# Splitting most FFN weight blocks by casting and accumulating transfers in a two-layer encoder trunk

## The chip, the cores and the metric

The kernel runs on one core of a Trainium2 chip. The time is device microseconds of one launch. The engines are TensorE (PE; PEld is its weight load), VectorE (DVE), ScalarE (ACT), GpSimd (POOL) and SyncE (SP). SP and POOL issue DMA transfers here: SP in both versions, POOL only in the changed one.

## The reference

Two layers of an encoder on a (512, 1024) float32 input. Each layer is a gated mixer of three attention-like branches, a layer norm, a SwiGLU FFN with 2816 hidden channels, and a second layer norm. The change touches the FFN alone:

```python
u = jnp.einsum('bsd,df->bsf', x, w_ffn_in[l])
u_gate, u_up = jnp.split(u, 2, axis=-1)
ffn = jnp.einsum('bsf,fd->bsd', jax.nn.silu(u_gate) * u_up, w_ffn_out[l])
x = _layer_norm(DEEPNORM_ALPHA * x + ffn, ln2_g[l], ln2_b[l])
```

## The kernel before

Every float32 matrix product is carried out as three products of float32r parts. A value w is split into a high part, w cast to float32r, and a low part, w minus the high part. `mm3` then multiplies high by high, high by low and low by high into one PSUM bank.

The program is a list of work items. An item has one or more weight blocks (`specs`) and a function that consumes them. A block is 1 MB of float32 weights, spread over 128 partitions with 2048 values each: for the FFN's input projection 8 row groups of 128 gate columns and 128 up columns (two pieces, in runs of 512 bytes), for its output projection 4 row groups of 512 columns (one piece, in runs of 2 KB). The sixth output block of each half has 2 row groups only.

`Wt` fetches and splits a block. SP loads it into one of two stage tiles `st`, ScalarE casts it to the high part `wh` in two halves, and VectorE subtracts `wh` from `st` to make the low part `wl`. `wh` and `wl` have four buffers each (`AHEAD`), so a block can be split as soon as TensorE has read the block four before it. `run_items` fetches ahead until four blocks are ready or in use, then runs the next item. All engines take their instructions in the order in which a scheduler has put them, and wait at the head of their queue.

In layer `l` the FFN consists of these items: `u_ffn_first(2)` with the first two input blocks, `u_ffn(2)` to `u_ffn(21)` with one input block each, `u_fout(0, 0..5)` and `u_fout(1, 0..1)` with one output block each, and `u_fout_last` with the last four. A full block is 48 matmuls of 512 columns on TensorE. After an input block, `ffn_done` forms the hidden channels: a tanh and a cast on ScalarE, three operations on VectorE. The norm ahead of the FFN (`normalise`) takes one power per 128 rows on POOL; the transposes of the normed rows (`px`) wait for it, and `u_ffn_first` needs them.

Of the kernel before, what the change touches and what calls it, by code (L numbers as in the profile page):

```python
# [12 lines left out]
F32R = mybir.dt.float32r  # L13
AF = mybir.ActivationFunctionType
ALU = mybir.AluOpType

P = 128
# [32 lines left out]
def trunk(ctx, tc, x_in, w_in, ret_norm_g, da_norm_g, lq1, lk1, lq2, lk2, w_a, w_b, w_c, b_merge, w_out,  # L50
          ln1_g, ln1_b, w_ffn_in, w_ffn_out, ln2_g, ln2_b, rel, rope_ret, rope_da, decay, out):
    nc = tc.nc
# [5 lines left out]
    wsp = ctx.enter_context(tc.tile_pool(name="wsp", bufs=AHEAD))  # L58
# [9 lines left out]
    def g(dt=F32, name="g"):  # L68
        return gp.tile([P, 512], dt, tag="g", name=name)

    def f(ap):
        return ap.bitcast(F32)

    def bank(name="ps"):
        return psp.tile([P, 512], F32, tag="ps", name=name)

    class Pair:


        def __init__(self, name="pr"):  # L80
            self.hi = g(F32R, name + "h")
            self.lo = g(F32R, name + "l")
# [23 lines left out]
    class Wt:  # L106


        def __init__(self, pieces, nk, meanwhile=None):
            ncol = sum(ap.shape[1] for ap in pieces)  # L110
            n = nk * ncol
            st = wst.tile([P, 2048], F32, tag="st", name="st")[:, :n].rearrange("p (k c) -> p k c", k=nk)
            hi = wsp.tile([P, 2048], F32R, tag="wh", name="wh")[:, :n]
            lo = wsp.tile([P, 2048], F32R, tag="wl", name="wl")[:, :n]
            c0 = 0
            for ap in pieces:
                w = ap.shape[1]
                src = ap.rearrange("(k p) c -> p k c", p=P)
                if meanwhile is None:
                    nc.sync.dma_start(st[:, :, c0:c0 + w], src)  # L120
                else:
                    for k in range(0, nk, 2):
                        nc.sync.dma_start(st[:, k:k + 2, c0:c0 + w], src[:, k:k + 2])
                c0 += w
            self.hi = hi.rearrange("p (k c) -> p k c", k=nk)
            self.lo = lo.rearrange("p (k c) -> p k c", k=nk)
            self.nk = nk
            h = max(nk // 2, 1) if meanwhile is None else 2
            for a in range(0, nk, h):
                b = min(a + h, nk)  # L130
                nc.scalar.copy(self.hi[:, a:b], st[:, a:b])  # L131
                nc.vector.tensor_sub(self.lo[:, a:b], st[:, a:b], f(self.hi[:, a:b]))  # L132
                if meanwhile is not None and a == 0:
                    meanwhile()

    def proj_T(act, wt, c0, nk=KT, ps=None, half=None):

        ps = bank("pt") if ps is None else ps
        sl = slice(0, S) if half is None else slice(256 * half, 256 * half + 256)
        for k in range(nk):  # L140
            a = act[k]
            mm3(ps[:, sl], wt.hi[:, k, c0:c0 + P], wt.lo[:, k, c0:c0 + P], a.hi[:, sl], a.lo[:, sl],
                k == 0, k == nk - 1)
        return ps
# [11 lines left out]
    def proj_N(act, wts, t, ps, k0=0, start=True, stop=True):  # L156

        sl = slice(P * t, P * t + P)
        rows = [(wt, k) for wt in wts for k in range(wt.nk)]
        for i, (wt, k) in enumerate(rows):  # L160
            a = act[k0 + i]
            mm3(ps, a.hi[:, sl], a.lo[:, sl], wt.hi[:, k], wt.lo[:, k], start and i == 0, stop and i == len(rows) - 1)

    def rows_of(w, c, k0=0, nk=KT):

        return [([w[P * k:P * min(k + 4, k0 + nk), c:c + 512]], min(4, k0 + nk - k)) for k in range(k0, k0 + nk, 4)]
# [80 lines left out]
    def bcast_rows(src):  # L247

        r = [g(name="bc") for _ in range(2)]
        for hf in range(2):  # L250
            nc.sync.dma_start(r[hf], src[:, 512 * hf:512 * hf + 512].to_broadcast([P, 512]))
        return r

    class Norm:
# [10 lines left out]
        def finish(self, t):  # L265

            mv = small.tile([P, 2], F32, tag="mv", name="mv")
            nc.vector.bn_aggr(mv, self.st[t])
            rs = small.tile([P, 2], F32, tag="rs", name="rs")
            nc.vector.tensor_scalar_add(rs[:, 0:1], mv[:, 1:2], LN_EPS)  # L270
            nc.gpsimd.tensor_tensor(rs[:, 1:2], rs[:, 0:1], mhalf[:, 0:1], op=ALU.pow)
            for z, gam in zip(self.z[t], self.gam):
                nc.vector.scalar_tensor_tensor(z, z, mv[:, 0:1], gam, op0=ALU.subtract, op1=ALU.mult)
            for hf, (z, bet) in enumerate(zip(self.z[t], self.bet)):
                nc.vector.scalar_tensor_tensor(z, z, rs[:, 1:2], bet, op0=ALU.mult, op1=ALU.add)
                nc.sync.dma_start(self.dst[P * t:P * t + P, 512 * hf:512 * hf + 512], z)
# [41 lines left out]

    items = []

    def item(specs, fn, *groups):

        items.append((specs, fn, groups))

    pending = []

    def between():

        if pending:
            for fn in pending.pop(0):  # L330
                fn()

    def run_items():
        ready, at = [], 0

        def fetch():
            nonlocal at
            specs, at = items[at][0], at + 1
            ready.append([])
            for sp in specs:  # L340
                first = at == 1 and not ready[-1]
                if first:
                    load_x(0, 2)
                ready[-1].append(Wt(*sp, meanwhile=first_x if first else None))

        for i, (specs, fn, groups) in enumerate(items):
            while at <= i or (at < len(items) and sum(map(len, ready)) < AHEAD):
                fetch()
            pending.extend(groups)
            fn(*ready.pop(0))  # L350
            while pending:
                between()
# [3 lines left out]
    def load_x(t0, t1):  # L356
        for t in range(t0, t1):
            start[t] = [g(name="xn") for _ in range(2)]
            load_rows(start[t], x_in[P * t:P * t + P])
# [10 lines left out]
    def layer(l):  # L370
# [436 lines left out]
        def load_res(src):  # L807
            x1["z"] = [[g(name="z") for _ in range(2)] for _ in range(NT)]
            for t in range(NT):
                load_rows(x1["z"][t], src[P * t:P * t + P])  # L810

        def u_out(hf):
# [29 lines left out]
            return rows_of(w_out[l], 512 * hf), fn  # L842

        item(*u_out(0))
        item(*u_out(1))


        hid = [None] * FT

        def ffn_spec(i):  # L850
            w = w_ffn_in[l]
            return ([w[:, P * i:P * i + P], w[:, FFN + P * i:FFN + P * i + P]], KT)

        def ffn_done(i, pg, pu):
            t = g(name="fth")
            nc.scalar.activation(t, pg, AF.Tanh, scale=0.5)  # L856
            nc.vector.scalar_tensor_tensor(t, t, 1.0, pg, op0=ALU.add, op1=ALU.mult)  # L857
            nc.vector.tensor_mul(t, t, pu)  # L858
            hid[i] = Pair("hid")
            split(hid[i], t, scale=0.5)  # L860
# [14 lines left out]
        def u_ffn(i):  # L875
            def fn(wt):
                pg = proj_T(x1T, wt, 0)
                pu = proj_T(x1T, wt, P)
                ffn_done(i, pg, pu)
            return [ffn_spec(i)], fn  # L880

        item(*u_ffn_first(2))
        for i in range(2, FT):
            item(*u_ffn(i))

        last = l == DEPTH - 1
        fo = {}
# [2 lines left out]
        def fout_done(hf, t):  # L890
            residual(x1["z"][t][hf], fo[hf][t])
            x2["n"].stats(t, hf)

        def u_fout(hf, kb):

            spec = rows_of(w_ffn_out[l], 512 * hf, 0, FT)[kb]

            def fn(wt):
                if kb == 0:
                    fo[hf] = [bank("pf") for _ in range(NT)]  # L900
                    if hf == 0:
                        load_res(saved[2 * l])
                        x2["n"] = Norm(x1["z"], v["g2"], v["b2"], bcast_rows(ln2_g[l:l + 1]),
                                       bcast_rows(ln2_b[l:l + 1]), xTs[l + 1], out if last else saved[2 * l + 1])
                for t in range(NT):
                    proj_N(hid, [wt], t, fo[hf][t], 4 * kb, kb == 0, 4 * kb + wt.nk == FT)
                    if 4 * kb + wt.nk == FT:
                        fout_done(hf, t)
            return [spec], fn
# [18 lines left out]

        nb = -(-FT // 4)
        for kb in range(nb):  # L930
            item(*u_fout(0, kb))
        for kb in range(nb - NLAST):
            item(*u_fout(1, kb))
        item(*u_fout_last(nb - NLAST))

        def hook(t):
# [9 lines left out]
    for l in range(DEPTH):  # L946
        layer(l)
    run_items()


# [44 lines left out]
```

## Time and profile before

| | |
|---|---|
| time, median of 2 runs | 1973.27 us (1973.19 to 1973.35) |
| profiled execution, its own time | 1973.74 us |
| its span, first to last instruction | 1972.0 us |
| TensorE busy, granted clock | 1953.1 us (99%), 0.998 |
| VectorE busy | 1045.0 us (53%) |
| ScalarE busy | 788.6 us (40%) |
| POOL busy | 48.2 us (2%) |
| moved by DMA, share of 16 engines | 201.67 MB, 32.3% |

The busy times are unions of what the profiler recorded for each engine. Matmuls overlap each other in the records, so that an engine that is always busy may still be fed late; the waits and the chain of work tell that. Times in the rows of a timeline are microseconds from the start of the span; "<-" names what ended a wait.

### The profile page before, as it was taken

The page shows a single profiled execution, that of the slowest core. Times are in us where ns is not written, and L with a number is a line of the kernel's source. Part 1 is how long each engine was busy: PE and PEld are TensorE (multiplying, and loading weights), DVE is VectorE, ACT ScalarE, POOL GpSimd, SP SyncE. Part 2 cuts the span into 40 slices and gives each one's busy share as a digit, 9 for nine tenths or more (in the row PEclk, how much of TensorE's full clock was granted, in tenths as well). Part 3 has the DMA queues.
Part 4 walks back from the last instruction along what each step waited for, and adds up shares of the span by engine and source line. Part 5 has one row for each costly group of instructions (what it writes and reads, how often), then busy time and mean ns, then how long its engine had stood idle before and what let it go on. Part 6 is the DMA issues. An engine that isn't in the chain of part 4 may idle for free.

```text
span 1972.0 us, 23963 instructions
## 1 busy us (share of the span) xinstructions
PE 1953.1 (99%) x9506; PEld 1647.8 (84%) x9506; DVE 1045.0 (53%) x1918; ACT 788.6 (40%) x1431; POOL 48.2 (2%) x73
## 2 busy tenths in 40 slices
PE   8999999999999999999999999999999999999998
PEld 7888888888888888888898888888888898888886
DVE  4664556577557434333375545655774684343333
ACT  4443445466534322221154434555674343232220
POOL 0000000000000000000000000000000000000000
PEclk9999999999999999999999999999999999999999
DMA  5421332232145333242143223232221633332421
GB/s 187 135 89 56 118 102 82 74 97 75 64 150 163 106 96 100 92 159 97 62 163 118 75 86 102 76 90 86 86 86 48 209 109 111 102 95 98 160 75 43
DMA packets 222197, 203.21 MB, mean 103 GB/s; under 512 B 6926, under 2 KB 179076, under 8 KB 222084
## 3 DMA queue, kind: packets, MB, share of 16 engines
q1 hardware_dynamic: 222084, 201.67, 32.3%
q8 instruction: 75, 1.23, 0.3%
q14 instruction: 38, 0.31, 0.0%
HBM read 193.26 MB, written 8.39 MB: 102 GB/s over the span
## 4 chain that ended last, share of the span: by engine, by line
PE 98%; DVE 1%; DMA 0%; issue 0%; ACT 0%; SPq 0%; POOL 0%; DVEq 0%; ACTq 0%
PE pt L102 20%; PE pt L104 20%; PE pt L103 20%; PE pn L102 5%; PE pn L104 5%; PE pn L103 5%; PE pf L104 4%; PE pf L102 4%; PE pf L103 4%; PE ptr L238 1%; PE pco L625 1%; PE psc L209 1%; PE psc L208 1%; PE pdo L698 1%; PE po L104 1%; PE po L103 1%
## 5 line engine op out<-in xcount | busy, mean ns | idle before, releaser
L102 PE MATMUL pt<-xTh,wh 128*128 128x512 f32 (+1 forms) x1600 | 599.1, 375 | 4.6 <-ACT xTh L86 3.5
L103 PE MATMUL pt<-xTl,wh 128*128 128x512 f32 (+1 forms) x1600 | 596.0, 373 | 0.2 <-DVE xTl L92 0.2
L104 PE MATMUL pt<-xTh,wl 128*128 128x512 f32 (+1 forms) x1600 | 595.7, 373 | 0.0
L132 DVE TENSOR_TENSOR wl<-st,wh 128x1024 fp32r<-128x1024 f32 (+1 forms) x346 | 391.3, 1152 | 269.2 <-ACT wh L131 264.1
L131 ACT CAST wh<-st 128x1024 fp32r<-128x1024 f32 (+1 forms) x346 | 334.7, 997 | 483.5 <-PE pt L103 279.5
L102 PEld LDWEIGHTS pt<-xTh,wh 128*128 128x128 f32 x1600 | 302.2, 189 | 56.6 <-ACT xTh L86 3.9
L104 PEld LDWEIGHTS pt<-xTh,wl 128*128 128x128 f32 x1600 | 301.9, 189 | 53.1
L103 PEld LDWEIGHTS pt<-xTl,wh 128*128 128x128 f32 x1600 | 302.4, 189 | 51.8 <-DVE xTl L92 0.5
L102 PE MATMUL pn<-wh,xTh 128*128 128x512 f32 x384 | 151.0, 393 | 0.5 <-ACT lnt L307 0.5
L103 PE MATMUL pn<-wl,xTh 128*128 128x512 f32 x384 | 149.6, 390 | 0.0
L104 PE MATMUL pn<-wh,xTl 128*128 128x512 f32 x384 | 149.6, 390 | 0.0
L102 PE MATMUL pf<-wh,hidh 128*128 128x512 f32 x352 | 137.1, 390 | 0.0
L104 PE MATMUL pf<-wh,hidl 128*128 128x512 f32 x352 | 137.0, 389 | 0.0
L103 PE MATMUL pf<-wl,hidh 128*128 128x512 f32 x352 | 136.9, 389 | 0.0
L858 DVE TENSOR_TENSOR fth<-fth,pt 128x512 f32<-128x512 f32 x44 | 30.2, 687 | 170.3 <-PE pt L104 170.3
L104 PEld LDWEIGHTS pn<-wh,xTl 128*128 128x128 f32 x384 | 72.1, 188 | 15.2
L102 PEld LDWEIGHTS pn<-wh,xTh 128*128 128x128 f32 x384 | 72.1, 188 | 14.8 <-ACT lnt L307 0.7
L103 PEld LDWEIGHTS pn<-wl,xTh 128*128 128x128 f32 x384 | 72.2, 188 | 14.0
L857 DVE SCALAR_TENSOR_TENSOR fth<-fth,pt 128x512 f32<-128x512 f32 x44 | 30.2, 687 | 91.5 <-ACT fth L856 91.5
L103 PEld LDWEIGHTS pf<-wl,hidh 128*128 128x128 f32 x352 | 66.1, 188 | 13.7
L104 PEld LDWEIGHTS pf<-wh,hidl 128*128 128x128 f32 x352 | 66.1, 188 | 13.7
L102 PEld LDWEIGHTS pf<-wh,hidh 128*128 128x128 f32 x352 | 66.1, 188 | 13.6
(180 smaller groups left out, 2421.5 us busy)
## 6 DMA issues: line engine op xcount, KB each, us to landing
st<-in_w_in SPq DMA_DIRECT2D x55, 1024.0 KB
st<-in_w_ffn_in SPq DMA_DIRECT2D x88, 512.0 KB
st<-in_w_ffn_out SPq DMA_DIRECT2D x20, 1024.0 KB
st<-in_w_in SPq DMA_DIRECT2D x32, 512.0 KB
st<-in_w_branch_a SPq DMA_DIRECT2D x8, 1024.0 KB
st<-in_w_out SPq DMA_DIRECT2D x8, 1024.0 KB
saved<-z SPq DMA_DIRECT2D x24, 256.0 KB
z<-saved SPq DMA_DIRECT2D x24, 256.0 KB
```

The costliest lines, as they stand in the source:

```text
L102: nc.tensor.matmul(ps, lh, rh, start=start, stop=False)
L103: nc.tensor.matmul(ps, lh, rl, start=False, stop=False)
L104: nc.tensor.matmul(ps, ll, rh, start=False, stop=stop)
L131: nc.scalar.copy(self.hi[:, a:b], st[:, a:b])
L132: nc.vector.tensor_sub(self.lo[:, a:b], st[:, a:b], f(self.hi[:, a:b]))
L208: nc.tensor.matmul(ps[:, :w], self.q[j][:, n], self.k[j][:, :w], start=True, stop=False)
L209: nc.tensor.matmul(ps[:, :w], self.q[j][:, n], self.kl[j][:, :w], start=False, stop=True)
L238: nc.tensor.transpose(ps[:, o + P * (nt - mt):o + P * (nt - mt) + P], E[pk][:, c + P * mt:c + P * mt + P], ident)
L625: nc.tensor.matmul(*x, start=mt == 0 and x is hi, stop=mt == NT - 1 and x is hi)
L698: nc.tensor.matmul(ps[:, 256 * j:256 * j + 256], pT[b].hi[:, o:o + P], vt[:, c:c + 256], start=mt == 0, stop=False)
L857: nc.vector.scalar_tensor_tensor(t, t, 1.0, pg, op0=ALU.add, op1=ALU.mult)
L858: nc.vector.tensor_mul(t, t, pu)
```

## The change

A second way to fetch and split a block is added, `WtDma`. It has no stage tile. POOL issues a transfer of the weights straight into `wh`; since the tile is float32r and the source float32, the transfer casts. ScalarE then writes the negative of `wh` into `wl` (one instruction over 2048 columns), and POOL issues a second transfer of the same weights that accumulates onto `wl`. The second half of this, `finish`, is called when the next block is fetched. `run_items` takes the way per item. `WtDma` is used for `u_ffn(2)` to `u_ffn(21)` of layer 1 only, and for `u_fout(0, 0..5)` and `u_fout(1, 0..1)` of both layers: 36 blocks in all. All others, the mixers' blocks among them, keep `Wt`.

```diff
+    class WtDma:
+        def __init__(self, pieces, nk):
+            ncol = sum(ap.shape[1] for ap in pieces)
+            n = nk * ncol
+            hi = wsp.tile([P, 2048], F32R, tag="wh", name="wh")[:, :n]
+            lo = wsp.tile([P, 2048], F32R, tag="wl", name="wl")[:, :n]
...
+            c0 = 0
+            for ap in pieces:
+                w = ap.shape[1]
+                src = ap.rearrange("(k p) c -> p k c", p=P)
+                nc.gpsimd.dma_start(self.hi[:, :, c0:c0 + w], src)
+                self.pieces.append((slice(c0, c0 + w), src))
+                c0 += w
+
+        def finish(self):
+            hi, lo = self.flat
+            nc.scalar.activation(lo, f(hi), AF.Copy, scale=-1.0)
+            for cols, src in self.pieces:
+                nc.gpsimd.dma_start(self.lo[:, :, cols], src, accum_op=ALU.add)
...
             for sp in specs:
                 first = at == 1 and not ready[-1]
                 if first:
                     load_x(0, 2)
-                ready[-1].append(Wt(*sp, meanwhile=first_x if first else None))
+                while open_:
+                    open_.pop().finish()
+                if make is None:
+                    ready[-1].append(Wt(*sp, meanwhile=first_x if first else None))
+                else:
+                    ready[-1].append(make(*sp))
+                    open_.append(ready[-1][-1])
...
         for i in range(2, FT):
-            item(*u_ffn(i))
+            item(*u_ffn(i), make=WtDma if l else None)
...
         for kb in range(nb):
-            item(*u_fout(0, kb))
+            item(*u_fout(0, kb), make=WtDma)
         for kb in range(nb - NLAST):
-            item(*u_fout(1, kb))
+            item(*u_fout(1, kb), make=WtDma)
```

POOL's queue before, from the end of layer 1's mixer to the last norm (`rsr` and `rs` are the powers of the norms, `kl` zeroed key tiles):

```order
L712 TENSOR_TENSOR rsr<-ss,mhalf 128x4
L191 MEMSET kl 64x512
L192 MEMSET kl 64x512
L712 TENSOR_TENSOR rsr<-ss,mhalf 128x4 x2
L283 TENSOR_TENSOR rs<-rs,mhalf 128x1 x4
L271 TENSOR_TENSOR rs<-rs,mhalf 128x1 x4
```

The same place in the changed kernel, as far as the fifth `WtDma` block or so of layer 1 (L310 is the power that was L283; L153 the casting transfers, L161 the accumulating ones; 128x8x128 is one of a block's two pieces):

```order
L310 TENSOR_TENSOR rs<-rs,mhalf 128x1 x2
L153 DMA wh<-in_w_ffn_in 128x8x128
L310 TENSOR_TENSOR rs<-rs,mhalf 128x1
L153 DMA wh<-in_w_ffn_in 128x8x128 x3
L310 TENSOR_TENSOR rs<-rs,mhalf 128x1
L161 DMA wl<-in_w_ffn_in 128x8x128 x4
L153 DMA wh<-in_w_ffn_in 128x8x128 x3
L161 DMA wl<-in_w_ffn_in 128x8x128 x2
L153 DMA wh<-in_w_ffn_in 128x8x128
L161 DMA wl<-in_w_ffn_in 128x8x128 x2
L153 DMA wh<-in_w_ffn_in 128x8x128 x2
L161 DMA wl<-in_w_ffn_in 128x8x128 x2
```

The third and the fourth power of the norm now stand behind one and four casting pieces; from there on the queue alternates between two casting and two accumulating pieces.

ScalarE's queue before, in the middle of layer 1's input projection (`fth` is the tanh of a block, `hidh` the cast of its hidden channels; the cast of `wh` is that of a block three or four ahead):

```order
L856 ACTIVATE fth_13651<-pt_13601 128x512
L131 CAST wh_13660<-st_13659 128x1024 x2
L88 ACTIVATE hidh_13655<-fth_13651 128x512
L856 ACTIVATE fth_13718<-pt_13668 128x512
L131 CAST wh_13727<-st_13726 128x1024 x2
L88 ACTIVATE hidh_13722<-fth_13718 128x512
```

And now (L889 is the tanh that was L856, L159 the negation):

```order
L889 ACTIVATE fth_13809<-pt_13759 128x512
L88 ACTIVATE hidh_13813<-fth_13809 128x512
L159 ACTIVATE wl_13821<-wh_13820 128x2048
L889 ACTIVATE fth_13874<-pt_13824 128x512
L88 ACTIVATE hidh_13878<-fth_13874 128x512
L159 ACTIVATE wl_13886<-wh_13885 128x2048
```

Two casts of a staged block have become one negation, which reads what a transfer has brought; the tanh of the next block stands behind it.

More of the change, by code (lines that the diff above doesn't have):

```diff
@@ L134, in __init__ @@
                     meanwhile()
+    class WtDma:
[4 more added lines that the diff above has]
+            lo = wsp.tile([P, 2048], F32R, tag="wl", name="wl")[:, :n]
+            self.hi = hi.rearrange("p (k c) -> p k c", k=nk)
+            self.lo = lo.rearrange("p (k c) -> p k c", k=nk)
+            self.flat = hi, lo
+            self.nk, self.pieces = nk, []
+            c0 = 0
[10 more added lines that the diff above has]
+                nc.gpsimd.dma_start(self.lo[:, :, cols], src, accum_op=ALU.add)
     def proj_T(act, wt, c0, nk=KT, ps=None, half=None):
@@ L319, in trunk, with item @@
     items = []
-    def item(specs, fn, *groups):
-        items.append((specs, fn, groups))
+    def item(specs, fn, *groups, make=None):
+        items.append((specs, fn, groups, make))
     pending = []
@@ L333, in run_items @@
     def run_items():
-        ready, at = [], 0
+        ready, at, open_ = [], 0, []
         def fetch():
             nonlocal at
-            specs, at = items[at][0], at + 1
+            specs, make, at = items[at][0], items[at][3], at + 1
             ready.append([])
@@ L343, in fetch @@
                     load_x(0, 2)
-                ready[-1].append(Wt(*sp, meanwhile=first_x if first else None))
-        for i, (specs, fn, groups) in enumerate(items):
+                while open_:
[5 more added lines that the diff above has]
+                    open_.append(ready[-1][-1])
+        for i, (specs, fn, groups, _) in enumerate(items):
             while at <= i or (at < len(items) and sum(map(len, ready)) < AHEAD):
```

## Prediction

> **What bounds the kernel now.** I read the page's busy table and its chain first, then the list of TensorE's waits, then the busy time of the stretch that the change touches most.
>
> ```profile
> span 1972.0 us, 23963 instructions
> PE 1953.1 (99%) x9506; PEld 1647.8 (84%) x9506; DVE 1045.0 (53%) x1918; ACT 788.6 (40%) x1431; POOL 48.2 (2%) x73
> PE 98%; DVE 1%; DMA 0%; issue 0%; ACT 0%; SPq 0%; POOL 0%; DVEq 0%; ACTq 0%
> ```
>
> The last line is the chain that ended last: TensorE is 98% of it. The profiled execution took 1973.74 us, 1.7 more than its span and 0.5 more than the median of the two timed runs (1973.27), so I work from 1973.74. TensorE's waits are few:
>
> ```profile
> PE px L294 <- DMA xn<-in_x: 4.5, 2, 3.7
> PE pt L102 <- ACT xTh L86: 3.5, 2, 3.2
> PE psc L208 <- DVE ocl L94: 1.1, 2, 0.6
> PE pt L102 <- DVE z L805: 1.1, 2, 0.6
> PE pn L102 <- ACT lnt L307: 0.5, 1, 0.5
> PE pt L102 <- DVE dPl L92: 0.3, 2, 0.2
> PE pt L103 <- DVE xTl L92: 0.2, 1, 0.2
> 1660.00:1850.00 190.00, 190.00 (x840) 157.30 (x840) 77.18 (x89) 55.36 (x71) 0.00 (x0) 1.00 0.36 109
> ```
>
> They add up to 11.2 us, and none names a weight tile (`wh`, `wl`) as what was late. The last row is a stretch of layer 1's FFN (start and end, length, then the busy time of PE, PEld, DVE, ACT, POOL, then clock, DMA share, GB/s): TensorE worked 190.00 of 190.00 us at clock 1.00. **There is nothing to win in this stretch**; the question is only whether the new way of splitting keeps up with it.
>
> **What goes.** Blocks 2 to 21 of layer 1's input projection (20) and 8 output-projection blocks in each layer (16, two of them half-sized) no longer pass the stage tile: about 72 half-block casts and 72 subtractions.
>
> ```profile
> L132 DVE TENSOR_TENSOR wl<-st,wh 128x1024 fp32r<-128x1024 f32 (+1 forms) x346 | 391.3, 1152 | 269.2 <-ACT wh L131 264.1
> L131 ACT CAST wh<-st 128x1024 fp32r<-128x1024 f32 (+1 forms) x346 | 334.7, 997 | 483.5 <-PE pt L103 279.5
> ```
>
> That is 72 x 1.15 = 83 us off VectorE and 72 x 1.0 = 72 us off ScalarE, which gets 36 negations back. VectorE is 53% busy and TensorE doesn't wait for either in this stretch, so I credit 0. Nothing hides less than before on these two engines.
>
> **What comes: a chain through POOL.** The order of instructions shown above has POOL's queue alternate: two casting transfers of block b, then its two accumulating ones, then the casting ones of b+1. The accumulating ones wait for the negation on ScalarE, which waits for the casting ones to land; b+1's casting ones stand behind them. So each block passes one serial chain. TensorE's need per block:
>
> ```profile
> 1643.47 0.60 ACT L856 ACTIVATE fth<-pt 128x512 f32<-128x512 f32 x1 [3.13 <-PE pt L104]
> 1654.35 0.60 ACT L856 ACTIVATE fth<-pt 128x512 f32<-128x512 f32 x1 [3.13 <-PE pt L104]
> 1598.81 1.06 ACT L131 CAST wh<-st 128x1024 fp32r<-128x1024 f32 x1 [0.57 <-PE po L104]
> 1627.01 1.05 ACT L131 CAST wh<-st 128x1024 fp32r<-128x1024 f32 x1 [2.16 <-PE pt L103]
> 1637.81 2.01 ACT L131 CAST wh<-st 128x1024 fp32r<-128x1024 f32 x2 [4.62 <-PE pt L103]
> ```
>
> The tanh of one block follows that of the one before by 1654.35 - 1643.47 = **10.88 us**, which is TensorE's time per block. The third row shows when the buffer of block 2 comes free (TensorE has read it), the fourth that of block 5, when TensorE starts block 2. The fifth gives two 1024-column casts in 2.01 us; I take 2.0 us for one 2048-column negation.
>
> Now the links of the chain. How a plain block load runs today:
>
> ```profile
> 1706.60 33.63 SPq L120 DMA_DIRECT2D st<-in_w_ffn_in  x8
> GB/s 0 0 0 0 0 0 0 0 0 0 0 0 0 0 37 88 143 127 72 82 229 305 322 338 336 340 350 334 293 295 262 170 66 6 0 0 0 0 0 0
> DMA packets 2080, 1.05 MB, mean 105 GB/s; under 512 B 32, under 2 KB 2080, under 8 KB 2080
> L120 SPq DMA_DIRECT2D st<-in_w_ffn_in x88: 367/474/1684, 580.0 to 1783.2; - x88
> ```
>
> The second row cuts 1704 to 1714 us into 40 slices: the block issued from 1706.60 on begins to move at 1707.5, 0.9 us later, and 1.05 MB in 512-byte runs are over at about 1712.4. At the 300 GB/s of the later slices, 1.05 MB are 3.5 us. SP issues each of the two pieces (1024 runs) in a median 474 ns.
>
> POOL has no DMA in this trace, and **how long POOL takes to issue 1024 runs is the unknown that decides**. The nearest rows:
>
> ```profile
> L192 POOL MEMSET kl<- 64x512 f32 x16 | 8.5, 530 | 31.7 <-DVE mx L224 14.7 <-DVE rot L177 10.5 <-DMA tb<-in_rel 4.5
> masks.py:199 POOL TENSOR_SCALAR_AFFINE_SELECT ident<-ident 128x128 f32<-128x128 f32 x1 | 0.3, 285 | 0.0
> L984 POOL MEMSET const-float32-1.0<- 128x1 f32 x1 | 0.1, 103 | 0.0
> L283 POOL TENSOR_TENSOR rs<-rs,mhalf 128x1 f32<-128x1 f32 x12 | 10.4, 869 | 537.2 <-DVE rs L282 537.2
> L530 POOL TENSOR_TENSOR rsr<-ss,mhalf 128x4 f32<-128x4 f32 x8 | 8.1, 1012 | 283.4 <-DVE ss L529 283.4
> ```
>
> A POOL instruction costs about 0.1 us fixed (103 ns). A step per column costs (530 - 103) / 512 = 0.83 ns for a memset, (285 - 103) / 128 = 1.42 ns for the affine select, which works out an index per element, and (1012 - 869) / 3 = 48 ns for the power. Low end: POOL issues like SP, 0.47 us per piece. Far end: 48 ns per run, 49 us per piece, over 190 us per block and more than 3 ms in all; working out addresses is nothing like a power, so this end only says that the tail is long. I take the affine select as the nearest and one such step for each end of a run. A casting run has two ends (read, write): 0.1 + 1024 x 2.84 ns = **3.0 us per piece**. An accumulating run has three, since it also reads what it adds to: 0.1 + 1024 x 4.26 ns = **4.5 us per piece**.
>
> Chain per block: 2 x 3.0 issue + 1.0 until the last runs have landed (0.9 as above, rounded up) + 2.0 negation + 2 x 4.5 issue = **18.0 us** against 10.88. Data (3.5 us per transfer, or 7 if accumulating moves twice as much) runs behind the issue and adds nothing here.
>
> In a sentence of its own: the Trainium skill, "DMA: Bandwidth & Descriptors", section "Measured (HBM→SBUF, 128 partitions, SWDGE, issued from GpSimd)", gives 6.15 us for 1 MB moved from a POOL queue. An estimate by that figure for both transfers would be 6.15 + 2.0 + 6.15 = 14.3 us per block plus the waits between, some 60 to 90 us in all; no run here shows such a transfer yet.
>
> **The sum.** Times on the clock of before. POOL issues blocks 2 and 3 from 1598.8: four casting pieces and one power (0.9) end at 1611.7; their four accumulating pieces (18.0) end at 1629.7. Block 4: +6.0 +1.0 +2.0 +9.0 = 1647.7, landed 1648.7. TensorE wants block 4 at 1627.0 + 2 x 10.88 = 1648.8. The stock of loaded blocks is then used up, and blocks 5 to 21 come 18.0 - 10.88 = 7.1 us late each: 17 x 7.1 = **121 us**.
>
> Output-projection blocks are one piece of 512 runs of 2 KB: casting 1.6 us, accumulating 2.3 us by the same steps; here the data is the longer part:
>
> ```profile
> 830.00:831.00 1.00, 1.00 (x7) 1.00 0.74 254
> 831.00:832.00 1.00, 1.00 (x6) 1.00 1.03 401
> 832.00:833.00 1.00, 1.00 (x6) 1.00 0.93 358
> ```
>
> 1.0 MB in 2.9 us. Chain: 0.9 + 2.9 + 2.0 + 0.9 + 2.9 = 9.6 us, to 12.5 if accumulating moves twice as much; I take 12.0, 1.1 over TensorE's 10.88: about **8 us** for layer 1's eight. In layer 0 the first such block is wanted three blocks (32.6 us) after its buffer frees, 20 us more than its chain takes: **0**.
>
> Start of layer 1's FFN: POOL's powers of the norm now stand behind casting pieces that wait for a buffer.
>
> ```profile
> 1599.57 0.92 POOL L283 TENSOR_TENSOR rs<-rs,mhalf 128x1 f32<-128x1 f32 x1 [6.42 <-DVE rs L282]
> 1607.34 1.46 POOL L283 TENSOR_TENSOR rs<-rs,mhalf 128x1 f32<-128x1 f32 x1 [6.86 <-DVE rs L282]
> 1601.34 1.03 PE L294 MATMUL px<-ident,z 128*128 128x128 f32 x8
> 1610.46 1.03 PE L294 MATMUL px<-ident,z 128*128 128x128 f32 x8
> ```
>
> The third power would start at 1598.8 + 3.0 = 1601.8 instead of 1599.57 and the fourth at 1611.7 instead of 1607.34. The transposes `px` follow each by about 2 to 3 us with no slack, and TensorE stands behind them: **4 us**. ScalarE's two negations ahead of the second half's `lnt` end before those transposes and cost nothing.
>
> Sum: 121 + 8 + 4 = 133; 1973.74 + 133 = **2107 us**.
>
> Waiting also slows TensorE afterwards:
>
> ```profile
> 11.51 0.58 PE L102 MATMUL pt<-xTh,wh 128*128 128x256 f32 x1 [3.21 <-ACT xTh L86]
> 12.00:16.00 4.00, 3.79 (x18) 3.70 (x18) 2.48 (x5) 3.18 (x6) 0.00 (x0) 0.50 0.77 261
> 16.00:20.00 4.00, 4.00 (x31) 4.00 (x31) 3.92 (x7) 3.01 (x5) 0.00 (x0) 0.86 0.35 90
> ```
>
> After a wait of 3.21 us the granted clock was 0.50 for 4 us and 0.86 in the next 4. A block after a wait of 7.1 us would take some 2.5 us longer, 13.4: still under 18.0, so hidden in the next wait.
>
> **Rivals.** *POOL issues fast* (not slower): at SP's 0.47 us per piece the chain is 0.5 + 0.9 + 3.5 + 2.0 + 0.5 + 0.9 + 3.5 less 1.4 of the next issue, hidden behind data = 10.4 us, under 10.88: 1974 to 1980. It decides as long as the four issues of a block stay under 7.9 us (1.9 ns per run); within 2% (39 us, about what a measurement of this kernel can tell from no change) up to about 10 us. For it: SP's row. Against: SP's row is not POOL's work. A sentence apart: the Trainium skill, "DMA: Bandwidth & Descriptors", section "Anatomy of one DMA — SWDGE (gpsimd) path", says that many descriptors can be emitted before their cost shows, and that would end here; the trace cannot say, as POOL issues none.
>
> *Data bound*: fast issue, but accumulating reads two and writes one, 7 us of data; chain 10.4 + 3.5 = 13.9, 3.0 late. 17 x 3.0 and 8 x 3.0 less some 10 us of stock: 2040.
>
> *Dear runs*: POOL twice as slow as I took. Chain 12.0 + 1.0 + 2.0 + 18.0 = 33 us, 22 late per block: 17 x 22 = 374, with 40 for the rest 2390.
>
> *Faster*: would need waits that exist; all are 11.2 us, 0.6%, none on weights. The order of instructions has the transfers as announced, so that the change does nothing isn't one.
>
> **Numbers.** Forecast 2107 (2055 to 2250): 0.42. POOL fast: 0.20. Data bound: 0.13. Dear runs, 2250 and more: 0.24. Faster by over 2%: 0.01. Slower by over 2%: 0.42 + 0.13 + 0.24 = 0.79; within: 0.20. The range takes in the low end, 1974, and the dear case up to 2390; above are about 0.12.
>
> **What would show it.** POOL's issues should take about 3.0 and 4.5 us per piece; TensorE's new waits should be for the accumulating transfers into `wl`, about 7 us each, from block 5 of layer 1's input projection on, and none in layer 0's input projection. Layer 0's output projection should keep its time. I am wrong if a piece issues in under 2 us, if accumulating data rather than issue ends the wait, or if ScalarE's negation waits for something else than the casting transfer.

## The result, and the profile after

The changed kernel takes **2091.12 us** (median of 2 runs, 2089.44 to 2092.8) against 1973.27: 6.0% slower, ratio 1.0597 (95%: 1.0552 to 1.0643). The forecast was 2107, with 0.79 on slower by over 2%. The profiled execution took 2092.8 us, 119.1 more than that of before, where the sum said 133.

The page of the changed kernel, in the order of before: busy times, chain, POOL's DMA queue, and then the list of TensorE's waits (what waits, what was late, us in total, times, longest).

```profile
span 2091.0 us, 24033 instructions
PE 1986.4 (95%) x9506; PEld 1665.7 (80%) x9506; DVE 964.9 (46%) x1846; ACT 784.6 (38%) x1395; POOL 179.3 (9%) x185
PE 77%; DMA 10%; issue 8%; POOL 2%; ACT 2%; DVE 1%; SPq 0%; ACTq 0%; DVEq 0%; POOLq 0%
q0 software_dynamic: 99072, 73.41, 22.1%
PE pt L104 <- DMA wl<-in_w_ffn_in: 49.9, 15, 4.6
PE pf L103 <- DMA wl<-in_w_ffn_out: 34.2, 9, 11.0
PE pt L102 <- ACT lnt L334: 2.7, 1, 2.7
```

TensorE is 77% of the chain instead of 98%. It has three new waits, 86.8 us together: 15 times for the accumulating transfer of an input block, 9 times for that of an output block, and once at the start of layer 1's FFN. Its busy time grows by 1986.4 - 1953.1 = 33.3 us for the same 9506 matmuls, since the clock is lower after a wait: behind the wait of 4.63 us that ends at 1712.80 it was 0.65 from 1712 to 1715, 0.79 in the next 3 us, and then 1.00. Together that is 120.1 us, the whole 119 of the span within the overlap of the records. VectorE lost 80 us of work (83 forecast) and ScalarE 4 (0), which brought nothing.

The stretch of layer 1's FFN (a window; columns as in the prediction, with the DMA engines' share and GB/s at the end):

```profile
1660.00:1850.00 190.00, 155.55 (x635) 124.84 (x634) 22.03 (x33) 34.72 (x34) 57.91 (x48) 0.95 1.03 133
```

TensorE worked 155.55 of 190 us where it had worked 190.00, at clock 0.95.

Where the 119 us went is read from the first power of layer 1's norm, the first tanh of its FFN, and the first matmul of its output projection. First the three rows of before, then those of the changed kernel:

```profile
1585.34 0.55 POOL L283 TENSOR_TENSOR rs<-rs,mhalf 128x1 f32<-128x1 f32 x1 [69.49 <-DVE rs L282]
1618.48 0.60 ACT L856 ACTIVATE fth<-pt 128x512 f32<-128x512 f32 x1 [1.42 <-PE pt L104]
1844.55 0.39 PE L102 MATMUL pf<-wh,hidh 128*128 128x512 f32 x1
```

```profile
1595.53 0.55 POOL L310 TENSOR_TENSOR rs<-rs,mhalf 128x1 f32<-128x1 f32 x1 [69.49 <-DVE rs L309]
1633.03 0.60 ACT L889 ACTIVATE fth<-pt 128x512 f32<-128x512 f32 x1 [3.51 <-PE pt L104]
1930.05 0.39 PE L102 MATMUL pf<-wh,hidh 128*128 128x512 f32 x1
```

They are later by 10.2, 14.5 and 85.5 us, the end by 119.0. So layer 0's output projection lost **10.2** (0 forecast), the start of layer 1's FFN **4.4** (4), its input projection **71** (121), its output projection **33.5** (8).

**The chain itself.** Two negations on ScalarE and POOL's issues between them, in the middle of layer 1's input projection (start, duration, what it is, idle time before and what ended it), then the traffic from 1735.46 to 1755.46 in 40 slices of 0.5 us:

```profile
1735.46 1.92 ACT L159 ACTIVATE wl<-wh 128x2048 fp32r<-128x2048 f32 x1 [11.12 <-DMA wh<-in_w_ffn_in]
1751.10 1.92 ACT L159 ACTIVATE wl<-wh 128x2048 fp32r<-128x2048 f32 x1 [11.07 <-DMA wh<-in_w_ffn_in]
1737.68 3.16 POOL L161 DMA_DIRECT2D wl<-in_w_ffn_in  x2 [10.68 <-ACT wl L159]
1739.48 3.16 POOL L153 DMA_DIRECT2D wh<-in_w_ffn_in  x2
GB/s 0 0 0 0 0 0 0 0 0 74 152 181 183 182 182 164 167 165 166 171 178 244 328 359 334 306 291 245 93 30 0 0 0 0 0 0 0 0 0 0
```

The period is 15.6 us, against TensorE's 10.88. From one negation to the next: 2.2 us for the negation and until POOL answers it; 2.3 until the accumulating transfer moves its first bytes (slice 9, 1740.0); some 6.2 for its 1.05 MB at 165 to 185 GB/s; some 4.1 for the casting transfer of the next block, at about 300 to 360 GB/s (slices 21 to 29); 0.9 until the next negation. That the casting transfer moves only after the accumulating one is read from the step in the rate. Nothing moves in 5.4 of the 15.7 us that these make. The issues hardly count: POOL starts its third one 1.80 us after the first, so 0.9 us per piece; the recorded durations overlap.

### The profile page after: what moved, and what is told of

It reads as the page before. It is cut to its first block, busy times and chain, and to the rows that moved or that the text cites. A ratio compares the mean times of both kernels' runs of the same rounds, so it can differ in the third digit from the quotient of the medians.

```text
span 2091.0 us, 24033 instructions
## 1 busy us (share of the span) xinstructions
PE 1986.4 (95%) x9506; PEld 1665.7 (80%) x9506; DVE 964.9 (46%) x1846; ACT 784.6 (38%) x1395; POOL 179.3 (9%) x185
## 3 DMA queue, kind: packets, MB, share of 16 engines
q0 software_dynamic: 99072, 73.41, 22.1%
## 4 chain that ended last, share of the span: by engine, by line
PE 77%; DMA 10%; issue 8%; POOL 2%; ACT 2%; DVE 1%; SPq 0%; ACTq 0%; DVEq 0%; POOLq 0%
PE pt L102 16%; PE pt L104 16%; PE pt L103 16%; DMA wh<-in_w_ffn_in 7%; PE pn L102 5%; PE pn L103 5%; PE pn L104 5%; PE pf L103 2%; PE pf L104 2%; PE pf L102 2%; ACT wl L159 2%; PE ptr L265 1%; DMA wl<-in_w_ffn_in 1%; POOL wh L153 1%; POOL wl L161 1%
## 5 line engine op out<-in xcount | busy, mean ns | idle before, releaser
L104 PE MATMUL pt<-xTh,wl 128*128 128x512 f32 (+1 forms) x1600 | 605.1, 379 | 49.9 <-DMA wl<-in_w_ffn_in 49.9
L102 PE MATMUL pt<-xTh,wh 128*128 128x512 f32 (+1 forms) x1600 | 606.1, 380 | 6.6 <-ACT xTh L86 3.3
L103 PE MATMUL pt<-xTl,wh 128*128 128x512 f32 (+1 forms) x1600 | 602.9, 377 | 0.2 <-DVE xTl L92 0.2
L132 DVE TENSOR_TENSOR wl<-st,wh 128x1024 fp32r<-128x1024 f32 (+1 forms) x274 | 308.2, 1142 | 287.9 <-ACT wh L131 283.2
L104 PEld LDWEIGHTS pt<-xTh,wl 128*128 128x128 f32 x1600 | 306.5, 192 | 109.7 <-issue 55.8
L131 ACT CAST wh<-st 128x1024 fp32r<-128x1024 f32 (+1 forms) x274 | 263.6, 988 | 263.5 <-PE pt L103 163.9
L102 PEld LDWEIGHTS pt<-xTh,wh 128*128 128x128 f32 x1600 | 307.1, 192 | 60.0 <-ACT xTh L86 3.9
L103 PEld LDWEIGHTS pt<-xTl,wh 128*128 128x128 f32 x1600 | 306.8, 192 | 53.7 <-DVE xTl L92 0.5
L159 ACT ACTIVATE wl<-wh 128x2048 fp32r<-128x2048 f32 (+1 forms) x36 | 67.3, 1869 | 373.4 <-DMA wh<-in_w_ffn_out 156.6
L103 PE MATMUL pf<-wl,hidh 128*128 128x512 f32 x352 | 141.1, 401 | 34.3 <-DMA wl<-in_w_ffn_out 34.2
L103 PEld LDWEIGHTS pn<-wl,xTh 128*128 128x128 f32 x384 | 72.2, 188 | 13.9
L102 PEld LDWEIGHTS pf<-wh,hidh 128*128 128x128 f32 x352 | 67.9, 193 | 14.5
## 6 DMA issues: line engine op xcount, KB each, us to landing
wh<-in_w_ffn_out POOLq DMA_DIRECT2D x14, 1024.0 KB, 10.2
```

What stands on the lines that cost most here:

```text
L102: nc.tensor.matmul(ps, lh, rh, start=start, stop=False)
L103: nc.tensor.matmul(ps, lh, rl, start=False, stop=False)
L104: nc.tensor.matmul(ps, ll, rh, start=False, stop=stop)
L159: nc.scalar.activation(lo, f(hi), AF.Copy, scale=-1.0)
```

## The experiments

Theory A: the serial chain of a block through POOL's queue sets the period. Rival B: the DMA engines' throughput does. Rival C: POOL's issuing does.

**1. The next block's casting transfers ahead of this block's accumulating ones.**

```diff
-                nc.gpsimd.dma_start(self.lo[:, :, cols], src, accum_op=ALU.add)
+                tc.keep_in_program_order(nc.gpsimd.dma_start(self.lo[:, :, cols], src, accum_op=ALU.add))
...
-                while open_:
-                    open_.pop().finish()
                 if make is None:
                     ready[-1].append(Wt(*sp, meanwhile=first_x if first else None))
                 else:
                     ready[-1].append(make(*sp))
+                while open_:
+                    open_.pop().finish()
+                if make is not None:
                     open_.append(ready[-1][-1])
```

The accumulating transfers are also held to program order, so that the scheduler does not undo the swap. Holding alone wins nothing: run 7 below holds without swapping and takes 2109.01 us.

> The same transfers and negations, but POOL issues the casting transfers of the next block ahead of the accumulating ones of this block, so that a negation finds its high part landed a block earlier. Theory A (one serial chain per block: accumulating issue and data, then the next block's casting data, then landing, negation, 15.7 us in the changed kernel): the chain is cut, about 9.7 us of data per block are left against TensorE's 10.88, nearly no waits in the input projection, 1975 to 2000 us. Theory B (the DMA engines are simply too slow for twice the bytes): as the changed kernel, 2070 to 2095. Theory C (POOL's issue time): four issues per block as before, 2070 to 2095.

Measured: 1977.39 us (9 runs), ratio 1.0024 (1.0014 to 1.0034). The same window, POOL's issues, TensorE's last new wait, and the queue's total:

```profile
1660.00:1850.00 190.00, 190.00 (x840) 157.34 (x839) 37.24 (x54) 53.51 (x54) 79.81 (x65) 1.00 1.32 197
1694.82 1.80 POOL L153 DMA_DIRECT2D wh<-in_w_ffn_in  x2 [5.92 <-PE pt L104]
1696.58 3.22 POOL L161 DMA_DIRECT2D wl<-in_w_ffn_in  x2
PE pt L102 <- ACT lnt L334: 2.9, 1, 2.9
q0 software_dynamic: 99072, 73.41, 22.7%
```

The same 73.41 MB in the same 99072 packets through the same queue with the same negations, and TensorE is busy 190.00 of 190 us again. POOL now waits for a free buffer (`PE pt`), no longer for a negation. B and C fall. What is left of the loss in the profiled run, 2.7 us of its span (1974.7 against 1972.0), is the wait at the start of layer 1's FFN.

**2 and 3. Each half of the new way alone.** In the first, the casting transfer stays and VectorE makes the low part from a stage tile; in the second, ScalarE casts from a stage tile, and only the accumulating transfer stays.

```diff
 # casting alone
+                nc.sync.dma_start(st[:, :, c0:c0 + w], src)
                 nc.gpsimd.dma_start(self.hi[:, :, c0:c0 + w], src)
...
-            nc.scalar.activation(lo, f(hi), AF.Copy, scale=-1.0)
...
-                nc.gpsimd.dma_start(self.lo[:, :, cols], src, accum_op=ALU.add)
+                nc.vector.tensor_sub(self.lo[:, a:b], self.st[:, a:b], f(self.hi[:, a:b]))
 # accumulating alone
-                nc.gpsimd.dma_start(self.hi[:, :, c0:c0 + w], src)
+                nc.sync.dma_start(st[:, :, c0:c0 + w], src)
...
+                nc.scalar.copy(self.hi[:, a:b], self.st[:, a:b])
```

> The high part comes by POOL's casting transfer; the low part is made as before by VectorE from a stage tile that SP loads, so the bytes are still moved twice and POOL issues half as much. Theory A: no accumulating transfer, so no chain; 1973 to 1985 us. Theory B: twice the bytes, some 2030 or more. Theory C: half of the added time, about 2030.

> SP loads a stage tile, ScalarE casts it to the high part and writes the negation, and only the low part comes by POOL's accumulating transfer. The bytes are moved twice. Theory A: the negation waits for no transfer of POOL's, so accumulating transfers follow one another; 6.2 us of accumulating data and 3.5 of plain per block fit into 10.88; 1975 to 1990 us. Theory B (accumulating too slow, or too many bytes): 2040 to 2090. Theory C: about 2030.

Measured: 1976.11 us, ratio 1.0017 (1.0007 to 1.0027), and 1974.13 us, 1.0006 (0.9996 to 1.0016), 0.9 us under its range. TensorE is busy 190.00 us of the window in both. POOL's queue with casting alone, then with accumulating alone:

```profile
q0 software_dynamic: 49536, 36.70, 9.5%
```

```profile
q0 software_dynamic: 49536, 36.70, 13.2%
```

Neither half costs more than 0.3%; the loss comes with both on one queue. The same bytes keep the DMA engines busy 1.39 times as long when they accumulate.

**4 and 5. Input blocks alone, and output blocks alone.** In the first, all output blocks keep `Wt`; in the second, layer 1's input blocks do.

```diff
 # input blocks alone
-            item(*u_fout(0, kb), make=WtDma)
+            item(*u_fout(0, kb))
...
-            item(*u_fout(1, kb), make=WtDma)
+            item(*u_fout(1, kb))
 # output blocks alone
-            item(*u_ffn(i), make=WtDma if l else None)
+            item(*u_ffn(i))
```

> Only the 20 input-projection blocks of layer 1 go through the transfers; all output-projection blocks are split as before. The traces of the changed kernel put 4 us on the start and 71 on the input projection, 10 on layer 0's output projection and 33 on layer 1's. If these parts add up: 1974 + 75 = 2049 us (2040 to 2058). If layer 1's output projection lost time only because the input projection handed on an empty stock, the same; the next run tells that apart.

> Only the output projections of both layers pass POOL; layer 1's input projection is split as before the change. Theory A (one serial chain per block through POOL's queue; layer 1's output projection lost 33 us because the input projection handed it an empty stock): layer 0 loses its 10 us again, layer 1 starts with a stock like layer 0 and loses about 10 as well, so about 1994 us, and the start of layer 1's FFN loses nothing. Rival (an output block costs layer 1 its 33 us by itself, whatever came before): 1973 + 10 + 33 = 2016 us.

Measured: 2049.97 us, ratio 1.0390 (1.0369 to 1.0411), and 1996.35 us, 1.0116 (1.0085 to 1.0147). By their spans (2046.4 and 1997.1) they lose 74.4 and 25.1 us, 99.5 of the change's 119.0; some 20 are lost only when both are there. Output blocks alone: the first matmul of layer 1's output projection, and its waits for weights.

```profile
1855.84 0.39 PE L102 MATMUL pf<-wh,hidh 128*128 128x512 f32 x1
PE pf L103 <- DMA wl<-in_w_ffn_out: 19.6, 6, 7.8
```

The row is 11.3 us later than before, as the first power of layer 1's norm already is (1596.63); of the span's 25.1 us, 13.8 are layer 1's own. In the change they were 33.5, so 20 came from what the input projection handed on. One wait of the changed kernel shows how: TensorE begins output block 0, and at once stands for its low part.

```profile
1941.43 0.77 PE L103 MATMUL pf<-wl,hidh 128*128 128x512 f32 x1 [10.99 <-DMA wl<-in_w_ffn_out]
1925.52 3.64 SPq L272 DMA_DIRECT2D z<-saved  x8
1928.25 1.29 POOL L153 DMA_DIRECT2D wh<-in_w_ffn_out  x1
1945.42 1.92 ACT L159 ACTIVATE wl<-wh 128x2048 fp32r<-128x2048 f32 x1 [15.72 <-DMA wh<-in_w_ffn_out]
```

No split block is in stock here, and SP's loads of rows for the norm are moving at the same time; the negations before and after are 1945.42 - 1925.12 = 20.3 us apart. Run 5 has the same eight loads at the same point (from 1851.28) but a stock in hand: there the negations around them are 17.4 us apart (1844.98 and 1862.34), and TensorE does not wait for a weight before 1899. This points to the empty stock as what turns the long period into a wait here. That the loads make the period long is likely, but no run moved them.

**6. A longer chain: the negative written twice.**

```diff
-            nc.scalar.activation(lo, f(hi), AF.Copy, scale=-1.0)
+            [nc.scalar.activation(lo, f(hi), AF.Copy, scale=-1.0) for _ in range(2)]
```

> ScalarE writes each negative twice, 1.9 us more between the casting and the accumulating transfers of a block; bytes and transfers stay. Theory A (serial chain): the period of an input block goes from 15.7 to about 17.6 us; 1.9 us more for about 16 input blocks and 8 output blocks of layer 1 and some of layer 0's: 2137 to 2150 us. Theory B (the DMA engines' throughput sets the period) and theory C (POOL's issuing does): the idle time of DMA and of POOL takes it up, 2091 us as in the change.

Measured: 2094.29 us, ratio 1.0612 (1.0582 to 1.0643), where A had said 2137 to 2150. Taken alone, this speaks for B or C. The order on POOL tells otherwise. The changed kernel's is shown with the change; this is the order with the double negation, from the first accumulating transfers of layer 1 on:

```
L161 DMA wl<-in_w_ffn_in 128x8x128 x4
L153 DMA wh<-in_w_ffn_in 128x8x128 x4
L161 DMA wl<-in_w_ffn_in 128x8x128 x4
L153 DMA wh<-in_w_ffn_in 128x8x128 x2
L161 DMA wl<-in_w_ffn_in 128x8x128 x2
L153 DMA wh<-in_w_ffn_in 128x8x128 x3
```

After that it goes on two and two. The scheduler, which knew of the longer negation, moved one casting piece ahead for good (the `x3`): half a swap. Half of a casting block's 4.1 us leaves the chain and a second negation enters it, which would be about 15.7 again; the spacing is 1727.00 - 1710.91 = 16.1 and 1742.92 - 1727.00 = 15.9 us:

```profile
1710.91 3.87 ACT L159 ACTIVATE wl<-wh 128x2048 fp32r<-128x2048 f32 x2 [10.86 <-DMA wh<-in_w_ffn_in]
1727.00 3.86 ACT L159 ACTIVATE wl<-wh 128x2048 fp32r<-128x2048 f32 x2 [11.22 <-issue]
1742.92 3.86 ACT L159 ACTIVATE wl<-wh 128x2048 fp32r<-128x2048 f32 x2 [11.06 <-DMA wh<-in_w_ffn_in]
```

That the two cancel was read from the order afterwards; the next pair tests it. In the profiled run the input projection lost 74.5 us instead of 71. The output projections, whose order on POOL changed too, lost 18.1 us instead of 10.2 in layer 0 (first power of layer 1's norm at 1603.47) and 24.4 instead of 33.5 in layer 1, so that the nearness of the two totals is in part an accident.

**7 and 8. The same with POOL's order held.** The control holds POOL's transfers to program order; the second adds the double negation.

```diff
 # both
-                nc.gpsimd.dma_start(self.hi[:, :, c0:c0 + w], src)
+                tc.keep_in_program_order(nc.gpsimd.dma_start(self.hi[:, :, c0:c0 + w], src))
...
-                nc.gpsimd.dma_start(self.lo[:, :, cols], src, accum_op=ALU.add)
+                tc.keep_in_program_order(nc.gpsimd.dma_start(self.lo[:, :, cols], src, accum_op=ALU.add))
 # the second
-            nc.scalar.activation(lo, f(hi), AF.Copy, scale=-1.0)
+            [nc.scalar.activation(lo, f(hi), AF.Copy, scale=-1.0) for _ in range(2)]
```

> Control for the next run: POOL's transfers are held to strict alternation (two casting pieces, then that block's accumulating ones) from the first block on; in the change the first blocks have up to four casting pieces in a row. Theory A (serial chain): the period in the middle stays 15.7 us; less of a stock is built up at the start, so two or three more blocks come late by 4.8 us: 2095 to 2110 us. Theories B (throughput of the DMA engines) and C (POOL's issuing): 2091 us.

> The negative written twice as in the run before, but with POOL's transfers held to the order of the control, so that no casting piece of the next block slips ahead of a block's accumulating ones. Theory A: the period of an input block grows by the whole second negation, from 15.7 to about 17.6 us, and about 18 input and 15 output blocks are each 1.9 us later: 55 to 65 us above the control. Theories B and C: as the control, since traffic and issuing are the same.

Measured: 2109.01 us, ratio 1.0689 (1.0658 to 1.0720), and 2189.12 us, 1.1095 (1.1063 to 1.1128). The control lies 18 us above the change: without four casting pieces in a row at the start there is less stock to use up, and TensorE waits for 18 input blocks instead of 15. Negations of the control, then with the double one:

```profile
1703.01 1.92 ACT L159 ACTIVATE wl<-wh 128x2048 fp32r<-128x2048 f32 x1 [11.06 <-DMA wh<-in_w_ffn_in]
1718.82 1.92 ACT L159 ACTIVATE wl<-wh 128x2048 fp32r<-128x2048 f32 x1 [11.23 <-DMA wh<-in_w_ffn_in]
```

```profile
1711.67 1.92 ACT L159 ACTIVATE wl<-wh 128x2048 fp32r<-128x2048 f32 x1 [13.39 <-issue]
1714.01 1.90 ACT L159 ACTIVATE wl<-wh 128x2048 fp32r<-128x2048 f32 x1
1729.54 3.87 ACT L159 ACTIVATE wl<-wh 128x2048 fp32r<-128x2048 f32 x2 [10.97 <-DMA wh<-in_w_ffn_in]
```

15.8 us apart without, 17.9 with: the second negation goes into the period in full. The 80 us between the two runs are more than the 55 to 65 expected. Of the 77.5 between the profiled spans, 42 lie in layer 1's input projection (18 blocks by some 2.3 us, since a second negation often starts 2.3 us after the first, not 1.9), 16 in each output projection, and 4 at the start of layer 1's FFN, which the expectation had left out. Under B or C the idle time of the DMA engines or of POOL would have absorbed it.

**9. A shorter chain: each piece negated by itself.**

```diff
-            nc.scalar.activation(lo, f(hi), AF.Copy, scale=-1.0)
             for cols, src in self.pieces:
+                nc.scalar.activation(self.lo[:, :, cols], f(self.hi[:, :, cols]), AF.Copy, scale=-1.0)
                 nc.gpsimd.dma_start(self.lo[:, :, cols], src, accum_op=ALU.add)
```

> ScalarE negates each of a block's two pieces by itself, so that the first piece is negated while the second one is landing, and its accumulating transfer can be issued about 2 us earlier; order on POOL in the middle of the layer, bytes and transfers stay. Theory A: the period of an input block falls from 15.7 to about 13.3 us; output blocks are one piece and gain nothing; 16 x 2.4 = 38 us less: about 2050 to 2060 us. Theories B and C: 2091 us.

Measured: 2048.80 us, ratio 1.0382 (1.0352 to 1.0412), 1 us under the range expected. The first pieces' negations of two blocks:

```profile
1680.41 1.06 ACT L160 ACTIVATE wl<-wh 128x1024 fp32r<-128x1024 f32 x1 [7.95 <-DMA wh<-in_w_ffn_in]
1693.68 1.06 ACT L160 ACTIVATE wl<-wh 128x1024 fp32r<-128x1024 f32 x1 [8.04 <-DMA wh<-in_w_ffn_in]
```

The period is 1693.68 - 1680.41 = 13.3 us, as A said.

**10. The second transfer without accumulating.**

```diff
-                nc.gpsimd.dma_start(self.lo[:, :, cols], src, accum_op=ALU.add)
+                nc.gpsimd.dma_start(self.lo[:, :, cols], src)
```

> The second transfer overwrites wl instead of adding onto it (the low part is then the weight itself; the sum is left out). Order, waits and number of transfers stay; only what an accumulating transfer costs above a casting one goes. Theory A with 6.2 us of accumulating data against 3.7 of casting: the period falls from 15.7 to about 13.2 us, 16 x 2.5 us in the input projection and some 2.5 us for each output block that was late: 2015 to 2035 us. If accumulating costs no more than casting (the chain's excess lies in waits and fixed latencies alone): about 2091 us. If the accumulation were the whole cause: 1975 us.

Measured: 2004.45 us, ratio 1.0157 (1.0128 to 1.0187), 11 us below the range expected. Two negations, and TensorE's waits for weights:

```profile
1668.97 1.92 ACT L159 ACTIVATE wl<-wh 128x2048 fp32r<-128x2048 f32 x1 [9.75 <-DMA wh<-in_w_ffn_in]
1681.64 1.92 ACT L159 ACTIVATE wl<-wh 128x2048 fp32r<-128x2048 f32 x1 [9.75 <-DMA wh<-in_w_ffn_in]
PE pt L104 <- DMA wl<-in_w_ffn_in: 13.3, 10, 2.3
PE pf L103 <- DMA wl<-in_w_ffn_out: 7.4, 1, 7.4
```

This kernel leaves out the sum, so that the low part is the weight itself. The period is 12.7 us, 3.0 less. Output blocks are late once instead of nine times; I had counted that gain too low. Accumulating as such costs 87 of the 118 us, but only through the chain: with the swap of run 1 the same accumulating transfers cost next to nothing.

## Why the prediction was right, and where it was not

**The chain was right, what fills it was not.** One serial chain per block goes through POOL's queue, with the next block's casting transfers behind the accumulating ones; runs 1, 8 and 9 show it from three sides. The prediction filled it with issue, and it is made of data and waits for data. The forecast was 14 us above the profiled 2092.8, and that it came so near is luck: the input projection was forecast 50 us too high, the two output projections together 36 too low.

**The links of the chain were mis-sized, in opposite directions.** The sum gave 18.0 us per block, measured are 15.6. "2 x 3.0 issue" and "2 x 4.5 issue", 15 us, measured 4 x 0.9 = 3.6, nearly all of it beside data or the wait for first bytes. Data, which "runs behind the issue and adds nothing", measured 10.3 us per period. By the prediction's own test ("I am wrong if a piece issues in under 2 us, or if accumulating data rather than issue ends the wait") the price was wrong on both counts. The affine select was the wrong neighbour; SP's 0.47 us was the nearer row.

**The better forecast was half of a rival.** *Data bound* had fast issue and 7 us of accumulating data, period 13.9, 2040 us. Its data, 10.5 us, was nearly what was measured (10.3); its 3.4 us of all else were 5.4, since first bytes take 2.3 us instead of 0.9 and the last ones 0.9 to release the negation. It was given 0.13. Of *POOL issues fast* the premise held, 0.9 us per piece, and the conclusion didn't.

The Trainium skill, "DMA: Bandwidth & Descriptors", section "Anatomy of one DMA — SWDGE (gpsimd) path", says that many descriptors can be emitted before their cost shows; the trace agrees with four pieces of 1024 runs issued in 3.6 us (twice 1.80), yet the time did not follow it, as the chain was made of data. The estimate by the 6.15 us for 1 MB of the Trainium skill, "DMA: Bandwidth & Descriptors", section "Measured (HBM→SBUF, 128 partitions, SWDGE, issued from GpSimd)", was 14.3 us per block, nearer to the measured 15.6 than my 18.0. A casting transfer's data took 4.1 us here, an accumulating one's about 6.2.

**Term by term.** *Input projection*, 121 forecast, 71 measured: 15 blocks (7 to 21) came late by 15.6 - 10.88 = 4.7 us each, not 17 (from block 5 on) by 7.1. *Slower clock after a wait*: hidden in the next wait as forecast; TensorE's busy time grew 33.3 us inside periods that the chain set. *Layer 1's output projection*, 8 forecast: 13.8 by itself (run 5), since the period of a full block is 13.4 us in the changed kernel (1945.42 to 1958.85 on ScalarE; 13.1 for the next two) instead of 12.0, and 20 more from an empty stock. *Layer 0*, 0 forecast, 10.2: first and last of its eight negations,

```profile
841.10 1.92 ACT L159 ACTIVATE wl<-wh 128x2048 fp32r<-128x2048 f32 x1 [4.34 <-DMA wh<-in_w_ffn_out]
938.94 1.91 ACT L159 ACTIVATE wl<-wh 128x2048 fp32r<-128x2048 f32 x1 [11.40 <-DMA wh<-in_w_ffn_out]
936.23 0.77 PE L103 MATMUL pf<-wl,hidh 128*128 128x512 f32 x1 [7.42 <-DMA wl<-in_w_ffn_out]
```

lie 97.8 us apart, and TensorE needs 6.5 x 10.88 = 70.7 for the blocks between. The chain thus falls 27 us behind, more than the 20 us of stock; I had compared the stock with one chain instead of eight. The longest wait, the last row, follows the half-sized block, which TensorE finishes in half the time while the chain does not halve.

**The start was right by accident.** 4 us came, but not from POOL's powers. The fourth power follows the first by 1615.73 - 1595.53 = 20.2 us, before by 22.0:

```profile
1615.73 0.95 POOL L310 TENSOR_TENSOR rs<-rs,mhalf 128x1 f32<-128x1 f32 x1 [1.76 <-DVE rs L309]
1617.43 1.91 ACT L159 ACTIVATE wl<-wh 128x2048 fp32r<-128x2048 f32 x1 [5.38 <-DMA wh<-in_w_ffn_in]
1619.25 0.55 ACT L334 ACTIVATE lnt<-px,colv 128x256 f32<-128x256 f32 x1
1619.85 0.39 PE L102 MATMUL pt<-xTh,wh 128*128 128x256 f32 x1 [2.74 <-ACT lnt L334]
```

ScalarE's negation stood 5.38 us for its casting transfer, the last `lnt` behind it, and TensorE behind that; the prediction had said that these negations "cost nothing". The wait is there in runs 1, 4, 6, 9 and 10 as well (2.4 to 2.9 us), and gone in run 5, where no input block passes POOL.

## What to carry to other kernels

When two transfers of a block share an in-order queue and the second waits for an engine that waits for the first, their times add up even where the DMA engines could move more (run 1 moved the same bytes in TensorE's time), unless the next block's first transfer is queued ahead of this block's second. Price a chain by all its links, data and dead time included, and multiply it by the number of blocks before comparing it with a stock. And when an experiment changes a duration that a scheduler knows, look at the order it produced before reading the time: run 6 looked like a refutation and was a reordering.

## What the runs showed of the hardware

Accumulating transfers move at about half the rate of casting ones once they run. Output blocks alone, 40 slices of 1832 to 1852 us; an accumulating block of 2 KB runs comes first (about 205 GB/s), then a casting one (about 414):

```profile
GB/s 0 0 0 0 0 0 0 66 86 160 209 205 197 201 213 213 205 205 242 397 414 418 414 311 41 0 0 0 0 0 0 0 0 0 45 94 156 193 213 197
```

With 512-byte runs it is 165 to 185 against about 300 to 360, or some 6.2 us against 4.1 for 1.05 MB, and a casting transfer is no slower than a plain load of the same shape in the trace of before (300 to 350). POOL gets through 1024 runs in 0.9 us, casting or accumulating. From POOL's issue to the first bytes of an accumulating transfer about 2 us pass (1737.68 to 1740.0 with 512-byte runs, 1833.59 to 1835.5 with 2 KB runs), to those of layer 0's first casting one 1.5 (835.46 to 837.0), where SP's load in the trace of before took 0.9; from the last bytes to the negation that waits for them, 0.9.
